# The mean of squares of a delta-rule head: one plain float32 product, or two float32r products of a split pair

## The chip, the cores and the metric

The kernel runs on one core of a Trainium2 chip. The metric is device time of one execution in microseconds (us): the median over runs. One execution was also profiled; its instructions, waits and transfers are the trace. Engines are named as in the profile: PE (TensorE, matrix products), PEld (its weight loads), DVE (VectorE), ACT (ScalarE), POOL (GpSimd) and SP (SyncE, which here issues transfers).

## What is computed

One layer of a sequence model for 1024 tokens and 1024 channels, all in float32:

```
h   = rmsnorm(x);  P = h @ w_in                    # one input projection, its columns cut into parts
A   = gated delta rule, 8 heads of 128 channels, one scan per direction, the directions summed
      -> rmsnorm per head * silu(z) -> w_proj_gdn
B   = gated linear attention, 4 heads, both directions -> rmsnorm per head * silu(g) -> w_proj_gla
out = x + rmsnorm((sigmoid(ga) * A + sigmoid(gb) * B) @ w_out)
```

The change lies in A's norm: for each of the 8 heads and each token, the mean over the head's 128 channels of the squared output, and from it `(mean + eps) ** -0.5`. The 128 channels are on the 128 partitions, so the mean is a product with a 128 x 128 matrix whose every element is 1/128.

## The kernel before

**Stages.** First x is normalised and transposed (to about 60 us). Then come the 8 heads of the delta rule (to about 808 us), during which the next head's projections are computed; then the rest of the gates, the 4 heads of linear attention, the output projections and the last product.

**A head of the delta rule** has these parts, each a function below. `gdn_project` computes k, q and v of a head (products `pj_a`, L251), a convolution over five taps on VectorE (L506, L508) and z (`pj_z`). `gdn_decay` makes the factors `dt`: VectorE makes `xm` (L583), TensorE `pd` (L585) in the two PSUM banks of the pool `pacc`, ScalarE takes the exponential (L588). `gdn_inverse` forms the Gram products (`pgr`, L624), inverts the triangular blocks (a chain of 60 small steps on VectorE, L652 and L654, then small products L683 to L718), and prepares values and `pkq` (L738). `gdn_scan` is the recurrence over 8 chunks in both directions: `psc` (L779, L784, L794) on TensorE, `r`, `vd`, `S` on VectorE (L781, L787, L799), `vn` on ScalarE (L789), and the outputs `po` (L768), which lie in the same two banks as `pd`.

**The end of a scan**, where the change is: ScalarE squares the two halves of 512 tokens of `po` into `o` (L814), VectorE adds them to `osq` (L815), which already holds an eps term from q's norm; `rs_of` takes the mean of each half by a product with `o128` into the banks `s0` and `s1` (L473), then Ln (L478) and, for both halves, Exp (L479). `finish` multiplies z's gate by that root (L125), multiplies the outputs (L465) into `o`, and SP stores it (L466).

`rs_of` has two forms. With `pair` it splits its input: `split` lets ScalarE copy the values to float32r (L163) and VectorE take the difference from the original (L164), and two products of float32r follow (L476, L477). The linear attention uses that form, on halves of 512 tokens. With `None` it makes one product of float32 (L473); the trace shows such a product as two records of the same line. The delta rule uses that form.

**Buffers.** A tile's tag has a fixed number of slots. Tag `qe` has two of 128 x 1024 float32: per head first the queries times the decays of either direction (`qe`: loaded from DRAM, L749, then multiplied by q on VectorE, L750), then the squares `o`, which `finish` overwrites with the output. `pacc` has two banks, used in turn by `pd` of the head after the next and by `po` of the next head. `gt`, with two slots, holds parts of projections on their way to DRAM.

**Order.** The program is written head by head, but a planner orders it when the program is built: it runs a list by priorities (`at(...)`), with its own costs for each instruction, and fixes one order for each engine. An engine then works in that order and waits where an input or a slot is late. Inverse and decay factors come ahead of the scan of the head before, and projections (`P_FILL`) last, so that they fill what is free on TensorE. Beside the last head's scan 13 blocks of gates (`pj_t`) are the filling. SP's transfers, among them the weights (`raw`, L174), also have one order.

Of the kernel before, what the change touches and what calls it, by code (L numbers as in the profile page):

```python
# [32 lines left out]
# tiles of loaded weights, of their split parts, of x normalised, of padded projections  # L33
WRAW, WSPLIT, XS, XP = 2, 4, 4, 3
# the order in which a head's k, q and v are projected
A_ORDER = (1, 0, 2)
# the tiles of x that GpSimd scales, the weights whose low parts it takes
X_POOL = (1, 3, 5, 7)
LO_POOL = "azqv"
# blocks of the first projection's gates that are loaded ahead, and the head after whose states  # L40
GA_AHEAD, GA_HEAD = 2, 2
# gates computed beside a head's scan
# [6 lines left out]
# places in the schedule's order  # L49
# [8 lines left out]
def const_array():  # L58
    """Masks and the like: they depend on shapes alone."""
# [29 lines left out]
def layer_kernel(  # L89
# [23 lines left out]
    @contextmanager  # L113
    def at(priority):
        """what is emitted here comes in the schedule's order from this place on"""
        before = tc.cur_priority
        tc.cur_priority = priority
        yield
        tc.cur_priority = before
# [16 lines left out]
    def mm3(ps, lh, ll, rh, rl, n):  # L136
        """ps = (lh + ll)^T (rh + rl), summed over n pieces, without ll^T rl, which is
        below float32's last place."""
# [4 lines left out]
    # ------------------------------------------------------------ what lives throughout  # L143
# [16 lines left out]
    # ------------------------------------------------------------ split weights, projections  # L160
    def split(src, hi, lo):
        """src as a float32r pair whose sum is exact"""
        nc.scalar.copy(hi, src)  # L163
        nc.vector.tensor_tensor(lo, src, hi.bitcast(F32), op=ALU.subtract)  # L164

    def load_w(src, cols, name, g):
        """part of the rows of columns of a weight, [p, k, n], 512 elements of a partition;
        cols: list of (first column, width, place)."""
# [17 lines left out]
    # the weights' blocks in the order of their use: parts of them are loaded ahead  # L186
# [41 lines left out]
    def project_tokens(name, th, evac):  # L228
        """src^T w for half of the tokens: evac(b, psum) takes [128 tokens, (2 chunks, 256)]"""
        ps = [bank(pj, "pj", f"pj_{name}_{b}") for b in range(2)]  # L230
        for g in range(4):
            hi, lo = next_w(name, g)
            for b in range(2):
                for c in range(2):
                    ts = slice((2 * b + c) * P, (2 * b + c + 1) * P)
                    for k in range(2):
                        kk = 2 * g + k
                        for i, (a, w) in enumerate(((hh, hi), (hl, hi), (hh, lo))):
                            # the first product in a bank clears its marks of what is written
# [6 lines left out]
    def piece(ps, hi, lo, src, th, g, kn, cols=slice(0, 512)):  # L246
        """ps += what the g-th kn pieces of the rows bring, for columns of half of the tokens"""
# [7 lines left out]
    def project(name, evac, src=None):  # L255
        """rows of w^T src: evac(th, psum) takes [channels, 512 tokens]"""
# [8 lines left out]
    def in_steps(name, ps, gn):  # L265
        """as project, by quarters of the tokens"""
# [8 lines left out]
    def project_out(name, dst):  # L275
        """a block of channels kept in DRAM"""
# [13 lines left out]
    # ------------------------------------------------------------ constants of the two mixers  # L290
# [23 lines left out]
    def exp_ln_table():  # L314
        """after a function of another table: the one that has both exp and ln"""
# [4 lines left out]
    # ------------------------------------------------------------ h = rmsnorm(x), transposed  # L320
    with tc.tile_pool(name="xpool", bufs=2) as xpool:
# [23 lines left out]
        def scaled(t):  # L345
            """a tile of x normalised, its transpose"""
# [53 lines left out]
    # ------------------------------------------------------------ decays and gates of the scans  # L400
# [6 lines left out]
    def scan_gates(pool):  # L407
# [17 lines left out]
        # [tokens, direction, head, chunk]  # L425
# [19 lines left out]
        # exp of: the sums up to a token, of what is left of the chunk, of the whole chunk  # L445
# [15 lines left out]
    def finish(o_ps, wcol, rs, zs, o, dst, kc):  # L461
        """o * w * rs * zs, to its place in DRAM; zs is overwritten"""
# [5 lines left out]
    def rs_of(sq, pair, lhsT, eps, name, banks):  # L468
        """sq becomes (mean of sq over the channels + eps) ** -0.5; pair: room for sq as a float32r pair"""
        for i, b in enumerate(banks):  # L470
            pm = bank(*b, f"pm_{name}_{i}")
            if pair is None:
                nc.tensor.matmul(pm, lhsT=lhsT, rhs=sq[:, half(i)], start=True, stop=True)  # L473
            else:
                split(sq[:, half(i)], *pair)
# [678 lines left out]
```

## Time and profile before

| | |
|---|---|
| runs | 1585.59, 1590.22, 1590.51 us; median 1590.22 |
| the profiled execution | span 1591.5 us from its first to its last instruction; no other time of it is given |
| mean granted TensorE clock | 0.982 of full speed |
| busy: PE, PEld, DVE, ACT, POOL | 1526.6, 1283.3, 928.0, 673.1, 201.8 us |

The busy time of an engine is the union of its instructions' times. Products are pipelined, and the ends of their records are modelled, so that records overlap: a stretch of the chain of waits, which counts each moment once, shows how fast they follow one another. In the chain a piece gives its start, its length, the engine, the tile and the line.

### The profile page before, as it was taken

What the parts mean: (1) busy time and instruction counts of PE and PEld (TensorE: products, weight loads), DVE (VectorE), ACT (ScalarE), POOL (GpSimd) and SP (SyncE); (2) the same over time, 40 slices, a digit from 0 to 9 for tenths busy, and PEclk for the clock granted to TensorE, in tenths of its full rate; (3) what the DMA queues carried; (4) which work ended last, traced back from release to release, by engine and by line L of the source; (5) the groups of instructions that cost most, each with busy time, mean ns of one, the idle gap of its engine ahead of it and who ended that gap; (6) DMA issues with size and microseconds to landing.
All of it is one profiled execution on the core that took longest, in us unless ns stands there. A gap on an engine that the chain in (4) does not pass through costs nothing.

```text
span 1591.5 us, 25255 instructions
## 1 busy us (share of the span) xinstructions
PE 1526.6 (96%) x9622; PEld 1283.3 (81%) x9622; DVE 928.0 (58%) x2467; ACT 673.1 (42%) x1370; POOL 201.8 (13%) x225
## 2 busy tenths in 40 slices
PE   6998999999999999999999999999999999999998
PEld 6877787787878878787778898898888988787887
DVE  5497779979999899887511113314323355445413
ACT  5552535343444545453232325525436355433311
POOL 4242112111112121000000120110100100000000
PEclk9998999999999999998999999999999999999999
DMA  5221102121212121024143331231221335655404
GB/s 168 72 73 34 41 28 86 41 73 35 93 34 71 51 81 47 30 81 133 40 142 94 86 75 38 62 79 34 75 59 41 106 89 190 212 169 175 134 27 157
DMA packets 140882, 133.48 MB, mean 84 GB/s; under 512 B 11147, under 2 KB 114875, under 8 KB 140757
## 3 DMA queue, kind: packets, MB, share of 16 engines
q1 hardware_dynamic: 133282, 117.78, 25.0%
q10 hardware_dynamic: 6840, 12.00, 2.5%
q0 software_dynamic: 640, 2.10, 0.4%
q8 instruction: 75, 1.23, 0.3%
q14 instruction: 45, 0.37, 0.1%
HBM read 101.45 MB, written 30.39 MB: 83 GB/s over the span
## 4 chain that ended last, share of the span: by engine, by line
PE 62%; DVE 11%; DMA 6%; ACT 3%; issue 1%; SPq 1%; ACTq 0%; DVEq 0%
PE pj_t L251 9%; PE pj_y L251 7%; PE pj_v L240 6%; PE pout L141 5%; PE pj_a L251 5%; PE pj_g L251 5%; DVE tmp L652 3%; PE pj_q L251 3%; PE pj_k L251 3%; DVE yl L654 3%; PE pj_z L251 2%; PE po L768 2%; PE psb L946 2%; PE pob L968 2%; PE psc L794 1%; DMA st<-ob_d 1%
## 5 line engine op out<-in xcount | busy, mean ns | idle before, releaser
L251 PE MATMUL pj_a<-hh,hi_a 128*128 128x512 f32 x368 | 151.7, 412 | 0.0
L251 PE MATMUL pj_a<-hl,hi_a 128*128 128x512 f32 x368 | 151.0, 410 | 0.0
L251 PE MATMUL pj_a<-hh,lo_a 128*128 128x512 f32 x368 | 150.5, 409 | 0.0
L251 PE MATMUL pj_t<-hh,hi_t 128*128 128x512 f32 x256 | 103.9, 406 | 2.4 <-ACT gt L281 2.4
L251 PE MATMUL pj_t<-hh,lo_t 128*128 128x512 f32 x256 | 104.4, 408 | 0.0
L251 PE MATMUL pj_t<-hl,hi_t 128*128 128x512 f32 x256 | 104.3, 407 | 0.0
L181 POOL TENSOR_TENSOR lo_a<-raw_a,hi_a 128x512 fp32r<-128x512 f32 x48 | 68.6, 1430 | 235.1 <-ACT hi_a L177 224.9
L789 ACT ACTIVATE vn<-psc,c 128x128 f32<-128x128 f32 x128 | 45.0, 366 | 116.4 <-DVE vd L787 88.8
L652 DVE TENSOR_TENSOR tmp<-ulb,yl 128x54 f32<-128x54 f32 (+13 forms) x480 | 93.3, 235 | 1.3 <-DMA yl<-in_consts_dram 1.2
L654 DVE TENSOR_TENSOR yl<-yl,tmp 128x54 f32<-128x54 f32 (+13 forms) x480 | 90.9, 231 | 0.1
L251 PEld LDWEIGHTS pj_a<-hl,hi_a 128*128 128x128 f32 x368 | 71.1, 193 | 12.6 <-issue 1.0
L251 PEld LDWEIGHTS pj_a<-hh,lo_a 128*128 128x128 f32 x368 | 70.6, 192 | 12.8 <-issue 0.7
L251 PEld LDWEIGHTS pj_a<-hh,hi_a 128*128 128x128 f32 x368 | 70.6, 192 | 12.2 <-issue 0.7
L251 PE MATMUL pj_y<-ob,hi_y 128*128 128x512 f32 x256 | 79.1, 390 | 0.9 <-DVE gb L1073 0.9
L141 PE MATMUL pout<-wo,hh 128*128 128x512 f32 (+1 forms) x272 | 79.7, 377 | 0.0
L240 PE MATMUL pj_v<-lo_v,hh 128*128 128x256 f32 x256 | 72.4, 283 | 0.0
L240 PE MATMUL pj_v<-hi_v,hl 128*128 128x256 f32 x256 | 72.4, 283 | 0.0
L240 PE MATMUL pj_v<-hi_v,hh 128*128 128x256 f32 x256 | 72.4, 283 | 0.0
L181 POOL TENSOR_TENSOR lo_v<-raw_v,hi_v 128x512 fp32r<-128x512 f32 x32 | 41.3, 1290 | 231.9 <-ACT hi_v L177 226.1
L183 DVE TENSOR_TENSOR lo_t<-raw_t,hi_t 128x512 fp32r<-128x512 f32 x32 | 22.0, 689 | 64.1 <-ACT hi_t L177 64.0
L251 PEld LDWEIGHTS pj_t<-hh,hi_t 128*128 128x128 f32 x256 | 49.3, 193 | 12.2 <-ACT gt L281 2.8
L141 PEld LDWEIGHTS pout<-wo,hh 128*128 128x128 f32 x272 | 50.1, 188 | 9.4
(313 smaller groups left out, 4071.3 us busy)
## 6 DMA issues: line engine op xcount, KB each, us to landing
raw_a<-in_w_in_dram SPq DMA_DIRECT2D x48, 256.0 KB
qe<-eg_d SPq DMA_DIRECT2D x16, 512.0 KB
raw_t<-in_w_in_dram SPq DMA_DIRECT2D x32, 256.0 KB
gt_d<-gt SPq DMA_DIRECT2D x64, 128.0 KB
raw_v<-in_w_in_dram SPq DMA_DIRECT2D x32, 256.0 KB
xt<-in_x_dram SPq DMA_DIRECT2D x8, 512.0 KB
raw_z<-in_w_in_dram SPq DMA_DIRECT2D x16, 256.0 KB
z_d<-gz SPq DMA_DIRECT2D x32, 128.0 KB
```

Of the source, the lines that this page charges most:

```text
L141: nc.tensor.matmul(ps, lhsT=a(k), rhs=b(k), start=(s == 0), stop=(s == len(steps) - 1))
L181: nc.gpsimd.tensor_tensor(lo, raw, hi.bitcast(F32), op=ALU.subtract)
L183: nc.vector.tensor_tensor(lo, raw, hi.bitcast(F32), op=ALU.subtract)
L240: nc.tensor.matmul(ps[b][:, c * 256:(c + 1) * 256], lhsT=a[th][:, kk, ts], rhs=w[:, k, :], start=kk == 0 and i == 0 and c == 0, stop=kk == ...
L251: nc.tensor.matmul(ps[:, cols], lhsT=a[:, k, :], rhs=b[th][:, kk, cols], start=kk == 0 and a is hi and b is src[0], stop=kk == KD - 1 and ...
L652: nc.vector.tensor_tensor(tv, ul2[:, i, 0:i].unsqueeze(2).broadcast_to([P, i, w_]), yv[:, i].unsqueeze(1).broadcast_to([P, i, w_]), op=ALU ...
L654: nc.vector.tensor_tensor(yv[:, 0:i], yv[:, 0:i], tv, op=ALU.subtract)
L768: nc.tensor.matmul(po_n(n), lhsT=lhsT, rhs=rhs, start=count[b] == 1, stop=count[b] == len(todo[b]))
L789: nc.scalar.mul(vn[d], pc[d][:, P:2 * P], c1[:, d, n:n + 1])
L794: nc.tensor.matmul(pc[d][:, 2 * P:3 * P], lhsT=ktok[:, ns], rhs=vd[d], start=True, stop=True)
L946: nc.tensor.matmul(p_s[:, :256], lhsT=ktok[:, u], rhs=vt[:, n], start=True, stop=True)
L968: nc.tensor.matmul(po[e][:, j * P:(j + 1) * P], lhsT=a, rhs=b, start=(i == 0), stop=(i == len(todo) - 1))
```

## The change

The delta rule's mean is taken by the split form as well. `rs_of` loses its form without a pair. The pair of both halves is one new tile `pr` of tag `qe`: its first 512 columns are the high part and its last 512 the low part, of the first half and then of the second. The output gets a tile of its own, `on`, of the same tag, where before it overwrote the squares. So there are five users of the two slots per head where there were three. The matrix of 1/128 becomes float32r: a memset into a `gt` slot and a copy. The comments of the source are blanked out, which changes nothing that runs; lines below `rs_of` stand three earlier, those behind the end of `gdn_scan` one earlier, and those behind the constant one later.

```diff
     def rs_of(sq, pair, lhsT, eps, name, banks):
         for i, b in enumerate(banks):
             pm = bank(*b, f"pm_{name}_{i}")
-            if pair is None:
-                nc.tensor.matmul(pm, lhsT=lhsT, rhs=sq[:, half(i)], start=True, stop=True)
-            else:
-                split(sq[:, half(i)], *pair)
-                nc.tensor.matmul(pm, lhsT=lhsT, rhs=pair[0], start=True, stop=False)
-                nc.tensor.matmul(pm, lhsT=lhsT, rhs=pair[1], start=False, stop=True)
+            split(sq[:, half(i)], *pair)
+            nc.tensor.matmul(pm, lhsT=lhsT, rhs=pair[0], start=True, stop=False)
+            nc.tensor.matmul(pm, lhsT=lhsT, rhs=pair[1], start=False, stop=True)
             nc.scalar.activation(sq[:, half(i)], pm, AF.Ln, bias=eps_t[eps][:, 0:1])
         return nc.scalar.activation(sq, sq, AF.Exp, scale=-0.5)
...
         o = pool.tile([P, T], F32, tag="qe", name=f"o{h}", bufs=2)
         for g in range(2):
             nc.scalar.activation(o[:, half(g)], po[g], AF.Square)
             nc.vector.tensor_tensor(osq[:, half(g)], osq[:, half(g)], o[:, half(g)], op=ALU.add)
-        rs_of(osq, None, o128, "eq", f"a{h}", ((psc, "s0"), (psc, "s1")))
+        pr = pool.tile([P, T], F32R, tag="qe", name=f"pr{h}", bufs=2)
+        rs_of(osq, (pr[:, half(0)], pr[:, half(1)]), o128, "eq", f"a{h}", ((psc, "s0"), (psc, "s1")))
+        o = pool.tile([P, T], F32, tag="qe", name=f"on{h}", bufs=2)
         finish([(half(g), po[g]) for g in range(2)], gdn_w[:, 0:1], osq, zs[h], o, oa_d, h)
...
-        o128 = mconst.tile([P, P], F32, name="o128")
-        nc.gpsimd.memset(o128, 1.0 / 128)
+        o128 = mconst.tile([P, P], F32R, name="o128")
+        one = gpool.tile([P, 256], F32, name="one128", tag="gt")
+        nc.gpsimd.memset(one, 1.0 / 128)
+        nc.gpsimd.tensor_copy(o128, one[:, :P])
```

## Rows read from the trace of the kernel before

**Rows 1.** The page: span; busy us, share of the span, instructions.

```profile
span 1591.5 us, 25255 instructions
...
PE 1526.6 (96%) x9622; PEld 1283.3 (81%) x9622; DVE 928.0 (58%) x2467; ACT 673.1 (42%) x1370; POOL 201.8 (13%) x225
```

**Rows 2.** Windows of five heads, 268 to 704 us: busy us by engine, summed.

```profile
sum 436.00, PE 416.00 PEld 346.08 DVE 393.09 ACT 202.56 POOL 76.59; mean PE 83.20 PEld 69.22 DVE 78.62 ACT 40.51 POOL 15.32
```

**Rows 3.** TensorE's waits, 268 to 704 us: waited for, us, times, longest.

```profile
PE psc L794 <- ACT vn L789: 7.6, 6, 2.2
PE psc L779 <- DVE S L799: 4.5, 4, 2.2
...
PE pm_a L473 <- DVE osq L815: 1.0, 2, 0.8
PE pd L585 <- DVE o L465: 1.0, 1, 1.0
```

**Rows 4.** Windows of four head ends (394:441, 486:531, 561:612, 657:704), summed.

```profile
sum 190.00, PE 186.02 PEld 152.26 DVE 164.56 ACT 97.81 POOL 36.52; mean PE 46.51 PEld 38.06 DVE 41.14 ACT 24.45 POOL 9.13
```

**Rows 5.** The chain, behind the last head's scan: start, us, engine, tile, line, records.

```profile
802.05 1.99 PE pm_a L473 x4
...
824.59 75.35 PE pj_t L251 x324
```

**Rows 6.** Tile pm_a: count; ns min/median/max; first and last start us.

```profile
L473 PE MATMUL pm_a<-osq,o x32: 590/593/697, 236.6 to 803.4; 128*128 128x512 f32 x32
```

**Rows 7.** Tile pm_b, the same mean in the linear attention.

```profile
L476 PE MATMUL pm_b<-ob_hi,o x8: 394/496/501, 1017.0 to 1333.8; 128*128 128x512 f32 x8
...
L477 PE MATMUL pm_b<-ob_lo,o x8: 419/495/498, 1017.7 to 1335.9; 128*128 128x512 f32 x8
```

**Rows 8.** The chain at the head end of 306 us: the mean's products.

```profile
307.99 1.13 PE pm_a L473 x2
...
311.39 0.86 PE pm_a L473 x2
```

**Rows 9.** Tile ob_hi: the split in the linear attention.

```profile
L163 ACT CAST ob_hi<-sq x8: 615/617/636, 1016.3 to 1332.9; 128x512 fp32r<-128x512 f32 x8
L164 DVE TENSOR_TENSOR ob_lo<-sq,ob_hi x8: 691/692/1419, 1016.9 to 1335.1; 128x512 fp32r<-128x512 f32 x8
```

**Rows 10.** The chain at four head ends: its pieces on VectorE.

```profile
307.44 0.50 DVE osq L815
...
398.18 0.53 DVE osq L815
...
561.55 1.19 DVE k L508
...
562.92 0.60 DVE osq L815
...
737.86 0.75 DVE o L465
```

**Rows 11.** The end of 306 us: timeline, and the chain's load of decayed queries.

```profile
319.49 1.41 DVE L465 SCALAR_TENSOR_TENSOR o<-po,gdn_w,zs 128x512 f32<-128x512 f32 x2
...
325.67 0.48 PE L585 MATMUL pd<-xm,strict 128*128 128x256 f32 x2
...
330.05 4.33 DMA qe<-eg_d
...
341.43 0.38 PE L768 MATMUL po<-qe,S 128*128 128x128 f32 x2
```

**Rows 12.** VectorE's waits, 100 to 820 us.

```profile
DVE qe L750 <- DMA qe<-eg_d: 1.2, 3, 0.5
```

**Rows 13.** SP's waits, 100 to 820 us.

```profile
SPq L466 <- DVE o L465: 39.9, 5, 22.0
```

**Rows 14.** Window with a low clock: us, busy by engine, granted clock, DMA.

```profile
746.00:764.00 18.00, 18.00 (x159) 15.18 (x157) 5.01 (x9) 3.64 (x9) 0.52 (x1) 0.53 0.26 73
```

## The prediction

> **What bounds the kernel now.** I read the page's busy times first, then the windows by head, then what TensorE waits for, then the chain of waits at each head's end, then the tiles of the edited lines.
>
> The page [rows 1] shows TensorE busy for 96% of the span and VectorE for 58%. That mean mixes stages, and every edit but one lies at the ends of the delta rule's heads, so the windows there decide. Over five whole heads, 436 us, TensorE is busy 416.00 us (95%), VectorE 393.09 (90%), ScalarE 202.56 (46%) [rows 2]: two engines are nearly full at once, and TensorE leaves 4 us of the 87 us of a head. Its idle time, 20 us in the five, is mostly the scan's own ping-pong (7.6 and 4.5 us for psc); the mean's addition and the output's multiply hold it 1.0 us each [rows 3]. Four stretches from a scan's end to the next head's Gram products, where the edited code runs, are tighter still: TensorE 186.02 of 190 us (98%), VectorE 164.56 (87%), ScalarE 97.81 (51%) [rows 4]. So the reader is to see that TensorE's own work fills the place of the change, that VectorE has some 6 us of each 47 free there, and that ScalarE has half.
>
> Behind the eighth head's scan TensorE has projections in store (324 products in 75.35 us, merged into one piece of the chain [rows 5]), so a longer chain at that one end is covered.
>
> **The change part by part.** The profiled execution is known by its span, 1591.5 us [rows 1], 1.3 above the median of the runs, 1590.22; differences are worked out inside the span and set on the median.
>
> *Products.* A half head's mean of squares is one plain float32 product, which the trace shows as two records; two halves, four records, take 1.99 us on the path, so 1.00 us a half [rows 5]. It becomes two float32r products of 512 columns. The same shape in the dense stream takes 75.35 / 324 = 0.233 us [rows 5], a pair 0.47. A half gains 0.53 us, the 16 halves 8.5 us of TensorE time. The other bound comes from single records: 0.593 us each for the old ones [rows 6], 0.495 each for the linear attention's hi and lo products [rows 7], a gain of 2 x 0.098 = 0.2 a half, 3.1 in all. I take 0.53, because TensorE runs dense here and the stream is the nearest row. The chain of waits reaches back over the last seven head ends and holds nine of these halves there, the first two at 307.99 and 311.39 [rows 8], the last two in the 1.99 [rows 5]; on it the gain is 9 x 0.53 = 4.8 us.
>
> *Split.* Each half adds a ScalarE copy to float32r and a VectorE subtraction. The same lines at the same shape take 0.617 and 0.692 us in the linear attention [rows 9]: 16 x 0.617 = 9.9 us of ScalarE and 16 x 0.692 = 11.1 of VectorE. ScalarE's are covered by its half-idle time; without that cover they cost up to 9.9. VectorE's cost nothing where TensorE is the path and their whole time where VectorE is. The chain passes through VectorE around these lines at four of the seven ends [rows 10]: at 306 us only the first addition is on it, at 394 the second one leads to the product, at 562 both additions and a conv tap are on it, at 732 the output's multiplies. I count one, one, two and two subtractions: 6 x 0.692 = 4.2 us. At the other ends TensorE is the path. Bounds: 0 and 11.1.
>
> *One pair for both halves.* The second half's copy and subtraction overwrite the pair that the first half's two products read: a new wait of ScalarE and VectorE on TensorE. Behind ScalarE's copy stand the root's Ln and the scan's vn; behind VectorE's subtraction conv taps and the next scan. Its price is at most one product's time a head, 0.495 [rows 7], 4 us over eight, and 0 where other work is placed in between. I take 0, for both queues carry conv, inverse and projection work at that point, and keep 4.
>
> *Buffers.* The tag of the queries' decays has two slots. Now the squares take one, and the next head's first load takes the other at the scan's last step. After the change squares, pair and output come first in the program, so that the first load can wait for the pair's products; the second still waits for the output's store. At the end of 306 us the mean's last product ends at 311.39 + 0.86 = 312.25 [rows 8]; a load takes 4.33 us (330.05 to 334.38), and the scan's first product with a decayed query starts at 341.43 [rows 11]. The first load would land near 317, 24 us early; the second leaves 7 us for its multiply. I take 0. If a multiply stands too early in VectorE's order, the scan waits behind it: at most a landing, 4.3 us a head. VectorE waited for such loads 1.2 us in all [rows 12].
>
> On SP's queue the store stands ahead of weight loads, and SP waited 39.9 us for the output's multiply, at five of eight heads [rows 13]; a later multiply holds those loads by as much. Nothing in TensorE's waits is a weight load [rows 3], so 0.
>
> *The constant.* A memset at the start becomes a memset and a copy, in a slot that the projections' outputs use later. GpSimd does it long before the first mean's product at 236.6 [rows 6]: 0, at most a copy's 0.6 [rows 9].
>
> Sum: -4.8 + 4.2 = -0.6 us; 1590.22 - 0.6 = **1589.6 us**. A difference under 0.3%, 4.8 us, is about what a measurement of this kernel can't tell from no change.
>
> **Rivals.**
>
> *TensorE alone paces it.* If all subtractions fall into VectorE's free time, the whole 8.5 us of TensorE counts: 1581.7. For it: 98% at the head ends [rows 4], and TensorE's larger waits lie in the scan [rows 3]. Against: the VectorE pieces in the chain [rows 10].
>
> *VectorE paces the heads.* Then the 14 subtractions of the first seven ends lengthen them by their whole time, 14 x 0.692 = 9.7, and TensorE only waits longer: 1599.9. For it: 90% over whole heads [rows 2]; it decides once VectorE's 6 us per end are bound in waits for its inputs. Against: those 6 us, beside TensorE's 1.
> The Trainium skill (Perfetto Trace Analysis, "Identifying the Most-Contended Engine") speaks for this rival: matmul busy time is a poor measure of how near TensorE is to its limit, the share of weight loads is to be read instead, while VectorE's busy share may be taken as it is. By that rule TensorE stands at 346.08 of 436 us, 79%, below VectorE's 90% [rows 2], and the change relieves the wrong engine. The trace agrees in part: records of 0.593 us follow one another at 0.50 [rows 5, 6], so busy time overstates each record, though not that no gap is left between them.
>
> *The longer chain holds the decay factors.* The output's multiply frees the two PSUM banks that the decay factors of the head after next (pd) need, and the next scan's outputs wait for pd. Per head the chain gains two copies and two subtractions in series, 2 x 1.31, less 2 x 0.53: 1.6 us, and up to 2.4 more where each subtraction waits for a conv tap of 1.19 [rows 10]. Over six such ends that is 9 to 24 us; with 2 us each, 12: 1602. It decides where the delay exceeds the gap from the multiply's end to pd: 325.67 - 320.90 = 4.8 us at 306 [rows 11], none at 562, where pd waited for the multiply itself [rows 3].
>
> *The change doesn't do what it says.* The order is planned anew, from other product lengths and one more tile. A stretch where TensorE runs at 1.2 instead of 2.4 GHz, as in 746 to 764 us (mean granted clock 0.53 [rows 14], behind the inverse's small products), can come or go: up to half of its 18 us, 1581 to 1599, whatever the products save.
>
> **How the numbers follow.** The forecast, a cancelling, has 0.40: 0.34 of it within 0.3%, 0.04 faster, 0.02 slower. TensorE alone 0.27, faster. VectorE 0.11 and the chain 0.14, slower. The new plan 0.08: 0.04 faster, 0.03 the same, 0.01 slower. Faster 0.04 + 0.27 + 0.04 = 0.35; the same 0.34 + 0.03 = 0.37; slower 0.02 + 0.11 + 0.14 + 0.01 = 0.28. The likeliest case's own range, with 8.5 against nothing and 3.1 against 4.2 with 4 us of waits, is 1582 to 1595. Both signs hold much chance: below, the full 8.5 and half a clock drop, 1577; above, the chain's 12 us, 1603. The chain's far end and a split without any cover are left out.
>
> **What would show it.** The mean's four records of 1.99 us should shrink to under 1; 16 copies near 0.62 and 16 subtractions near 0.69 should appear, VectorE's busy time rising by 11 us. Forecast right: the five heads' 436 us stay within 3. TensorE alone: they shorten by 1 us each. VectorE: it is busy for 90% of longer heads. The chain: the time from the squares to pd grows, and TensorE waits for pd (L585) and the outputs after it. I am wrong if TensorE waits for decayed queries or weights, or if the time moves by over 13 us.

## The result, and the profile after

The kernel after takes 1612.59 us (median of 4 runs, 1610.07 to 1613.91), the kernel before, run beside it, 1589.44. The ratio is 1.014, 95% interval 1.0115 to 1.0165: by it, 22 us slower. The forecast was 1589.6 us, a cancelling of gain and cost; its likeliest range ended at 1595 and its widest at 1603. So it was wrong. In the experiments below, three of the twelve runs with subtractions alone (3793 to 8407 us) and one of the seven with the sum on TensorE (2467 us, the one that was profiled) took far longer than all others and are left out.

The page of the kernel after, its span and busy times (answers to [rows 1]):

```profile
span 1611.8 us, 25310 instructions
...
PE 1534.5 (95%) x9622; PEld 1292.7 (80%) x9622; DVE 937.4 (58%) x2483; ACT 695.2 (43%) x1396; POOL 202.5 (13%) x226
```

TensorE has as many instructions as before and is busy 8 us longer, though its products became shorter. ScalarE has 26 more, and only 16 of them are the copies of the split; the other 10 come up again at the end of the experiments. The windows say why TensorE is busy longer. The two heads in which most is lost, first before, from one head's Gram products to those of the head after next (us; busy by engine; granted clock; DMA share, GB/s):

```profile
440.80:611.70 170.90, 163.17 (x1267) 134.91 (x1266) 156.35 (x491) 79.99 (x175) 34.72 (x40) 1.00 0.20 60
```

and after:

```profile
442.90:626.70 183.80, 174.17 (x1276) 144.74 (x1276) 158.84 (x494) 87.96 (x184) 35.57 (x41) 0.94 0.19 55
```

The two heads take 12.9 us more. The third column from the end is the granted clock: 0.94, a rounded figure, over 183.80 us is 10 to 12 us lost, where before nothing was. So a reader of such a page must look at the clock before the engines' shares: at the lower level the same products take longer, and count as busy (projections of 512 columns follow one another at 0.43 us around 590 us, where the clock is 0.50, and at 0.23 at 600, where it is 1.00).

The instructions that replaced those of [rows 6], by tile, are as forecast in number and length (count; ns min/median/max; first and last start):

```profile
L163 ACT CAST pr<-osq x16: 604/618/628, 233.7 to 820.0; 128x512 fp32r<-128x512 f32 x16
L473 PE MATMUL pm_a<-pr,o x16: 392/398/628, 234.4 to 820.7; 128*128 128x512 f32 x16
L164 DVE TENSOR_TENSOR pr<-osq,pr x16: 679/692/1786, 234.5 to 820.6; 128x512 fp32r<-128x512 f32 x16
L474 PE MATMUL pm_a<-pr,o x16: 391/479/775, 236.3 to 821.4; 128*128 128x512 f32 x16
```

Their order in time isn't. The end of the fifth head in the timeline of the kernel after (start, us, engine, line; in brackets the idle time ahead of it and its releaser):

```profile
586.26 0.62 ACT L163 CAST pr<-osq 128x512 fp32r<-128x512 f32 x1 [0.76 <-DVE osq L812]
587.34 0.68 DVE L164 TENSOR_TENSOR pr<-osq,pr 128x512 fp32r<-128x512 f32 x1
...
590.65 0.63 PE L473 MATMUL pm_a<-pr,o 128*128 128x512 f32 x1
591.32 0.62 ACT L163 CAST pr<-osq 128x512 fp32r<-128x512 f32 x1 [1.35 <-PE pm_a L473]
...
595.64 0.78 PE L474 MATMUL pm_a<-pr,o 128*128 128x512 f32 x1
...
596.52 0.69 DVE L164 TENSOR_TENSOR pr<-osq,pr 128x512 fp32r<-128x512 f32 x1 [0.86 <-PE pm_a L474]
...
599.10 0.48 PE L474 MATMUL pm_a<-pr,o 128*128 128x512 f32 x1
```

The second copy waits for the first high product, the second subtraction for the first low product, and each product stands in TensorE's order behind others. The low half is ready at 588.0 and multiplied only at 595.64, so 9.2 us lie between the two subtractions. This is the longest of the ends, and TensorE ran at half speed from 581.6 to 598.7 us (its row stands in the last section), so part of those 9.2 us is the clock's. From the first square to the end of the output's multiply the first seven heads now take 12.4, 18.8, 19.4, 20.4, 23.8, 17.7 and 17.3 us, some 130 in all, where they took some 100.

TensorE's waits, 100 to 820 us (waited for; us, times, longest), answer to [rows 3] over a wider stretch; before, the largest were 11.7 for vn and 7.2 for xm:

```profile
PE psc L791 <- ACT vn L786: 15.9, 10, 2.4
PE pd L582 <- DVE xm L580: 9.2, 10, 3.1
PE po L765 <- DVE qe L747: 7.1, 1, 7.1
```

The third row is the wait for decayed queries that the prediction had named as a sign of its being wrong.

**One account for all kernels.** What lies behind the first product of the linear attention's queries takes 690 to 695 us in every kernel for which the account is given. Up to it the time splits into TensorE's idle time (the window less its busy time), what the lower clock costs (1 less the mean granted clock, times the span; the lower level is 1.2 of 2.4 GHz, and nearly all such stretches lie there), and the rest, TensorE's work at full clock. The window's row before, and after:

```profile
0.00:900.30 900.30, 847.03 (x5939) 704.82 (x5940) 674.89 (x2035) 392.87 (x838) 151.95 (x183) 0.97 0.24 71
```

```profile
0.00:918.70 918.70, 852.56 (x5939) 713.15 (x5940) 684.33 (x2051) 414.95 (x863) 152.62 (x184) 0.96 0.24 70
```

and the cores' row after, with the mean clock:

```profile
core 0: 1611.8 us, clock 0.974
```

| profiled execution | window | idle | lost to the clock | work at full clock |
|---|---|---|---|---|
| before (clock 0.982) | 900.3 | 53.3 | 28.6 | 818.4 |
| after (0.974) | 918.7 | 66.1 | 41.9 | 810.7 |

By this account the work shrank by 7.7 us, near the 8.5 of the dense stream in [rows 5]; 12.8 us of idle time and 13.3 us of clock stand against it. This split of the time is no finer than some 5 us, though: two kernels below that make the same products differ by 4.6 us in their work at full clock. Over all runs the clock tells the same: its mean is 0.9845 in the 97 runs of the kernel before that stand beside the experiments and 0.9765 in the 4 of the kernel after, that is 24.6 and 37.8 us.

### The profile page after: what moved, and what is told of

Same layout as the page of the kernel before. It is cut to its first block, busy times and chain, and to the rows that moved or that the text cites. A ratio compares the mean times of both kernels' runs of the same rounds, so it can differ in the third digit from the quotient of the medians.

```text
span 1611.8 us, 25310 instructions
## 1 busy us (share of the span) xinstructions
PE 1534.5 (95%) x9622; PEld 1292.7 (80%) x9622; DVE 937.4 (58%) x2483; ACT 695.2 (43%) x1396; POOL 202.5 (13%) x226
## 4 chain that ended last, share of the span: by engine, by line
PE 49%; DMA 5%; DVE 3%; ACT 3%; issue 1%; SPq 0%; ACTq 0%; DVEq 0%
PE pj_t L251 9%; PE pj_y L251 8%; PE pj_v L240 6%; PE pout L141 5%; PE pj_g L251 5%; PE pj_k L251 3%; PE pj_q L251 2%; PE pob L969 2%; PE psb L947 2%; DMA gt_d<-gt 1%; PE pc L901 1%; DMA raw_o<-in_w_out_dram 1%; DVE yl L651 1%; PE po L765 1%; PE pa L932 1%; DVE tmp L649 1%
## 5 line engine op out<-in xcount | busy, mean ns | idle before, releaser
L251 PEld LDWEIGHTS pj_a<-hh,hi_a 128*128 128x128 f32 x368 | 71.9, 195 | 11.5 <-ACT xp L491 0.2
L791 PE MATMUL psc<-vd,ktok 128*128 128x128 f32 x224 | 45.8, 295 | 16.1 <-ACT vn L786 15.9
L791 PEld LDWEIGHTS psc<-vd,ktok 128*128 128x128 f32 x224 | 35.0, 193 | 29.4 <-ACT vn L786 27.0
```

What stands on the lines that cost most here:

```text
L251: nc.tensor.matmul(ps[:, cols], lhsT=a[:, k, :], rhs=b[th][:, kk, cols], start=kk == 0 and a is hi and b is src[0], stop=kk == KD - 1 and ...
L791: nc.tensor.matmul(pc[d][:, 2 * P:3 * P], lhsT=ktok[:, ns], rhs=vd[d], start=True, stop=True)
```

## The experiments

All ratios are to runs of the kernel before beside them; brackets hold 95% intervals.

**Moving the pair out, and the buffers alone.** Four kernels. The first two put the pair into the slots of the keys by tokens:

```diff
-        pr = pool.tile([P, T], F32R, tag="qe", name=f"pr{h}", bufs=2)
+        pr = pool.tile([P, T], F32R, tag="ktok", name=f"pr{h}", bufs=2)
```

in the kernel after, with the output over the squares, and in the kernel before, with a copy and a subtraction of each half that nothing reads.

> The split and its two products as in the changed kernel, but the pair lies in the two slots of the tokens' keys (ktok), and the output overwrites the squares again; so the slots of the decayed queries have three users, as before. If the late loads of the decayed queries (five users of two slots) cost the 20 us: 1583 to 1594, as the split alone gives back TensorE's 8.5 us. If the longer chain in front of the decay factors' banks does: 1604 to 1613, the decay factors again starting where the output's multiply ends. If VectorE's and ScalarE's extra time does: 1604 to 1613 as well, but with the multiply no later after the squares than before.

> The kernel before with the 16 copies and 16 subtractions of the split added in the slots of ktok, at the same place, but nobody reads the pair: the plain product reads the sum as before. If VectorE's and ScalarE's time costs it: 1600 to 1613. If the late loads or the longer chain does: 1588 to 1597.

Measured: 1690.21 us, 1.0641 [1.062, 1.0663], and 1701.35, 1.0716 [1.0668, 1.0763]. Neither expectation was near. In both, the second head's Gram products start 5.6 us after the first head's first square; in the kernel before they start 63 us ahead of it. So the heads no longer overlapped. The slots are handed out in the program's order, and the next head's inverse, which writes its keys there, had to wait for this head's end. The two tell what that overlap is worth, some 100 us, and nothing of the change.

The third gave the kernel before five users of the decayed queries' two slots and no added instruction: the sum goes to a tile of its own, from which the plain product reads, and the output to another.

```diff
-            nc.vector.tensor_tensor(osq[:, half(g)], osq[:, half(g)], o[:, half(g)], op=ALU.add)
+            nc.vector.tensor_tensor(pr[:, half(g)], osq[:, half(g)], o[:, half(g)], op=ALU.add)
...
+        o = pool.tile([P, T], F32, tag="qe", name=f"on{h}", bufs=2)
```

> The kernel before with the five users of the two slots alone: the sum of squares is written to a tile in a slot of the decayed queries, the plain float32 product reads it there, and the output has a tile of its own. No instruction is added. If the late loads cost it: 1600 to 1613. If the longer chain or the added engine time does: 1586 to 1594.

Measured: 1589.32 us, 1.0005 [0.9987, 1.0024], idle time 53.3 us and clock 0.982 as before. That is in the range for the longer chain or the engines' time: the slots alone cost nothing. Its order of instructions was planned anew too, and differs from that of the kernel before in many places, so a new order by itself need not cost either.

The fourth gave the decay factors other banks in the kernel after, those of the Gram products:

```diff
-                pd = bank(pacc, f"o{g}", f"pd{h}_{d}_{g}")
+                pd = bank(pg, "g", f"pd{h}_{d}_{g}")
```

> The changed kernel, but the decay factors' products go to the two general PSUM banks (pg), so that they need not wait for the output's multiply; the next scan's outputs still do. If the longer chain in front of the decay factors costs it: 1585 to 1598. If the late loads do: 1603 to 1613, the scan's first outputs still standing behind the second load's multiply. If engine time does: 1603 to 1613 too, without such a wait.

Measured: 1625.58 us, 1.0228 [1.0199, 1.0256], slower still and outside both ranges. The factors no longer need the output's multiply, but they now share the inverse's banks; inconclusive.

**The split's work, and the chain's length.** From the kernel before, the copies and subtractions are added over the squares' buffer, read by nothing; then the subtractions alone.

```diff
+        for g in range(2):
+            hi = o[:, half(g)].bitcast(F32R)
+            split(osq[:, half(g)], hi, hi)
```

> The kernel before with the split's 16 copies and 16 subtractions added at the same place, now over the squares' own buffer (both parts into the same half, nobody reads them), so that no slot is shared in another way than before; the plain product reads the sum as before. If the engines' added time costs the 22 us: 1602 to 1614. If the longer chain up to the decay factors' banks does: 1588 to 1597.

> From the kernel before, with the 16 subtractions on VectorE alone added over the squares' buffer, not read by anything (no copies on ScalarE). With copies and subtractions both it was 1596.99 us, 9 above the kernel before. Theory 'VectorE's time costs it': 1594 to 1598 us. Rival 'ScalarE's time costs it': 1588 to 1590 us.

Measured: 1596.99 us, 1.0064 [1.0045, 1.0083], and 1593.77, 1.0023 [1.0004, 1.0043]. The first lies at the upper end of the range for the longer chain and below that for the engines' time; the second lies between its two ranges, nearer to VectorE's. The subtractions cost 3.7 us (0.0023 of 1590), the copies some 6 on top, though the intervals all but touch. So ScalarE's half-idle time was no full cover. Nor is this engine time alone: the output's multiply writes over the same buffer and has to wait for the idle split.

Then only the length of the chain: a GpSimd copy of each half between sum and plain product.

```diff
+            nc.gpsimd.tensor_copy(o[:, half(g)], osq[:, half(g)])
```

> The kernel before with nothing on VectorE and ScalarE, but with GpSimd copying each half of the sum over the squares before the plain product reads it from there: the chain gets longer by some 1.5 to 3 us a head. If the longer chain costs it: 1598 to 1614. If the engines' added time does: 1586 to 1593.

Measured: 1609.68 us, 1.0134 [1.0098, 1.017], inside the range for the longer chain. So a chain made longer, with no pair, no shared buffer and nothing added to VectorE or ScalarE, can cost as much as the whole change. But its seven ends lengthened by 10.4 us in all, those of the kernel with idle splits by 20.7, which lost half as much: the length of an end doesn't tell the time.

**Who pays for the pair.** The high part alone (the mean is that of the rounded squares, the low part is left out), then a pair for each half, with six users of the two slots:

```diff
-            split(sq[:, half(i)], *pair)
-            nc.tensor.matmul(pm, lhsT=lhsT, rhs=pair[0], start=True, stop=False)
-            nc.tensor.matmul(pm, lhsT=lhsT, rhs=pair[1], start=False, stop=True)
+            nc.scalar.copy(pair[i], sq[:, half(i)])
+            nc.tensor.matmul(pm, lhsT=lhsT, rhs=pair[i], start=True, stop=True)
```

```diff
+        pl = pool.tile([P, T], F32R, tag="qe", name=f"pl{h}", bufs=2)
+        rs_of(osq, [(pr[:, half(g)], pl[:, half(g)]) for g in range(2)], o128, "eq", f"a{h}", ((psc, "s0"), (psc, "s1")))
```

> The changed kernel without the low part: one copy to float32r and one product per half, halves in their own places (the mean of the squares is then taken of rounded squares). TensorE saves 0.77 us a half, no subtraction, no wait of the second half for the first. If the chain through the subtraction and the shared pair costs it: 1578 to 1592. If the late loads do, with ScalarE's copy: 1600 to 1610. If VectorE's time does: 1578 to 1592 too, which f2 and f5 tell apart.

> The changed kernel with a pair for each half (high parts in one tile, low parts in another, six users of the two slots): same instructions, but the second half's split does not wait for the first half's products, which stand behind the inverse's products in TensorE's order. If that wait makes the chain long: 1586 to 1600, the decay factors starting 3 to 6 us sooner after the scan. If the chain is long by the split itself or the engines' time costs it: 1604 to 1614.

Measured: 1581.37, 0.9958 [0.9937, 0.9978], and 1599.15, 1.0059 [1.0035, 1.0082]. Both are where the theory of the shared pair had them. The second does the change's whole computation, with no wait for a buffer of the first half, and most of the loss is gone. The same place in its timeline, here at full clock:

```profile
574.81 1.14 ACT L163 CAST pr<-osq 128x512 fp32r<-128x512 f32 x2
575.47 1.29 DVE L164 TENSOR_TENSOR pl<-osq,pr 128x512 fp32r<-128x512 f32 x2
...
579.79 0.71 PE L475 MATMUL pm_a<-pl,o 128*128 128x512 f32 x2
```

Both copies, both subtractions and both low products now run as pairs.

Next, the last head. In the kernel after its loads of the decays are issued at 785.78 us behind the next layer's transfers, and the 7.1 us of waiting follow. Issued from ScalarE's queue instead, with the shared pair and with a pair for each half:

```diff
-            nc.sync.dma_start(qe, eg_d[d, h:h + 1, :].broadcast_to([P, T]))
+            (nc.scalar if h == HA - 1 else nc.sync).dma_start(qe, eg_d[d, h:h + 1, :].broadcast_to([P, T]))
```

> The kernel after, with one thing changed: the eighth head's two loads of the queries' decays are issued from ScalarE's queue, so that they don't stand on SP's queue behind the next layer's transfers (in the trace of the kernel after they are issued at 785.78 us, behind transfers that wait for the step before; the product po of the last head waits 7.1 us for the multiply of the decayed queries, and the granted clock is low for 10.2 us after 786.4). Theory 'the late loads of the last head are one piece of the loss': about 1603 to 1606 us, the wait of po for the decayed queries gone and the stretch of low clock at 786 us gone. Rival 'the whole loss lies in the shared pair, this wait only moves idle time that is lost anyway': 1610 to 1614 us.

> The kernel after with a pair of its own for each half (six users of the queries' decays' buffers) and the last head's two loads issued from ScalarE's queue. If both pieces are there and add (13 us from the shared pair, about 9 from the late loads), the whole loss of 22 us is given back: 1587 to 1593 us. If the late loads are no piece of their own: 1597 to 1600 us, as with the pair for each half alone (1599.15).

Measured: 1611.15, 1.0142 [1.0115, 1.0169], and 1595.19, 1.0022 [1.0001, 1.0043]. The wait shrank to 3.0 us and the total did not move (1.014 before it): that theory fell. The second lies between its two ranges; with it, two kernels without sharing are at 1.0022 and 1.0059.

Now one index apart from the pair for each half: the high parts apart, one low part for both halves.

```diff
-        rs_of(osq, [(pr[:, half(g)], pl[:, half(g)]) for g in range(2)], o128, "eq", f"a{h}", ((psc, "s0"), (psc, "s1")))
+        rs_of(osq, [(pr[:, half(g)], pl[:, half(0)]) for g in range(2)], o128, "eq", f"a{h}", ((psc, "s0"), (psc, "s1")))
```

> The kernel after with a high part of its own for each half (ScalarE's second copy waits for no product), while both halves still share one low part (VectorE's second subtraction waits for the first half's low product). Same six users of the decayed queries' two buffers as with a pair for each half. If sharing the low part costs, through VectorE's wait: 1603 to 1611 us. If only ScalarE's wait on the high part costs (6 us for the high part alone, 1589.04 against 1581.37): 1592 to 1600 us, as with a pair for each half.

Measured: 1610.6 us, 1.0117 [1.0094, 1.0139], as expected if sharing the low part costs. The program has the same instructions and the same users of the slots; only the second subtraction must wait for the first low product. That is 0.0058 above the pair for each half, 9 us. The planned orders differ more than the edit: ScalarE runs 1396 instructions here, as in the kernel after, and 1388 with a pair for each half. Its window and the other's, and their clocks:

```profile
0.00:917.00 917.00, 849.23 (x5938) 709.20 (x5939) 683.87 (x2051) 414.26 (x863) 151.55 (x184) 0.96 0.24 70
```

```profile
core 0: 1612.0 us, clock 0.977
```

```profile
0.00:893.60 893.60, 832.62 (x5938) 692.85 (x5939) 684.96 (x2051) 403.71 (x855) 149.34 (x184) 0.98 0.24 72
```

```profile
core 0: 1585.3 us, clock 0.990
```

Idle time 67.8 against 61.0 us, the clock's loss 37.1 against 15.9, work at full clock 812.1 against 816.7. (This profiled execution of the pair for each half is its fastest; over all runs the mean clocks are 0.9798 and 0.9857, 32.4 against 22.8 us, 9.6 of the 11.5 between the medians.) So most of these 9 to 11 us are paid in clock, not in waits.

The counterpart, one high part for both halves, without a low part:

```diff
-                nc.scalar.copy(pair[i], sq[:, half(i)])
-                nc.tensor.matmul(pm, lhsT=lhsT, rhs=pair[i], start=True, stop=True)
+                nc.scalar.copy(pair[0], sq[:, half(i)])
+                nc.tensor.matmul(pm, lhsT=lhsT, rhs=pair[0], start=True, stop=True)
```

> The high part alone, but both halves use one buffer of 512 columns, so that the second half's copy on ScalarE waits for the first half's product (in the form that gave 1581.37 us each half has its own). If ScalarE's wait on a shared buffer is what the shared pair costs: 1588 to 1600 us. If it is the wait of VectorE's subtraction, or the length of the whole chain of two copies and two subtractions: 1580 to 1585 us.

Measured: 1589.04, 0.9997 [0.9979, 1.0014]; 0.0039 or 6 us above its form with two buffers and inside the range for a shared buffer, with intervals that just miss each other (0.9978 and 0.9979). Sharing costs there too, and takes the form's whole gain.

**Where the longer chain binds.** In the trace of the kernel after, the decay factors start at the very end of the output's multiply at all six ends that such factors follow, which speaks for the rival of the longer chain; but with a pair for each half they do so too, and most of the loss is gone there. The multiply can be taken off the chain at no cost in instructions: `finish_early` multiplies the outputs by the weight and z's gate as soon as the squares are summed, over the squares, which frees the banks; `finish_late` multiplies by the root and stores.

```diff
+        finish_early([(half(g), po[g]) for g in range(2)], gdn_w[:, 0:1], zs[h], o)
...
-        finish([(half(g), po[g]) for g in range(2)], gdn_w[:, 0:1], osq, zs[h], o, oa_d, h)
+        finish_late(osq, o, oa_d, h)
```

> From the kernel before, with the output's multiply taken apart: as soon as the squares are added up, VectorE multiplies the scan's outputs by the weight and by z's gate, out of PSUM and over the squares, and multiplies by the root afterwards, in SBUF. The number of VectorE's instructions is the same; the two PSUM banks that the decay factors of the head after next need come free before the mean's product instead of behind its whole chain. Theory 'the loop of banks paces the heads' (scan's outputs, squares, mean, root, output's multiply, decay factors, next scan's outputs): in the kernel before the decay factors start at the very end of the multiply at three or four of seven ends, so some of the loop is bound there too: 1575 to 1586 us. Rival 'the engines' queues pace the heads, the loop has slack': 1588 to 1594 us.

> The kernel after, split and one shared pair and two float32r products as they are, with the output's multiply taken apart in the same way (the output lies over the squares again). Theory 'the loop of banks': the pair's chain is no longer in the loop, and most of the 22 us is given back: 1580 to 1595 us. Rival 'the waits of ScalarE's and VectorE's queues for the shared pair hold what stands behind them': those waits stay, 1606 to 1614 us.

> The high part alone (a copy and one float32r product a half, the mean is that of rounded squares; 1581.37 us before) with the output's multiply taken apart in the same way. Theory 'the loop of banks': as the kernel before with the early multiply, less the products' saving, 1568 to 1580 us. Rival 'the queues': no gain from it, 1579 to 1586 us.

Measured: 1580.57, 0.9945 [0.9927, 0.9963] from the kernel before; 1603.22, 1.0105 [1.0065, 1.0145] from the kernel after; 1579.29, 0.9938 [0.9916, 0.996] with the high part alone. The first is as the theory of the banks had it; the second lies between its two ranges; the third fits either. The early multiply is worth 9 us to the kernel before. It gives the kernel after no more than that, and 1.05% of loss stays, 1.6% against the kernel before with the same edit: the banks aren't where the change costs. Another loop came into view. Rows of SP and VectorE in the timeline of the kernel after with the early multiply:

```profile
517.28 0.32 SPq L474 DMA_DIRECT2D oa_d<-o  x1
...
523.59 0.38 SPq L754 DMA_DIRECT2D qe<-eg_d  x1
...
529.08 1.23 DVE L755 TENSOR_TENSOR qe<-qe,q 128x1024 f32<-128x1024 f32 x1 [3.82 <-DMA qe<-eg_d]
```

The next head's second load waits for the store, VectorE for the load, and the scan's small steps stand behind; TensorE waited 11.7 us for decayed queries. The last multiply's output was therefore put over z's gate, so that the slot comes free at 517 instead of with the store's landing:

```diff
-        pool_mul(o, rs, o)
-        nc.sync.dma_start(dst[:, kc], o)
+        pool_mul(zs, rs, o)
+        nc.sync.dma_start(dst[:, kc], zs)
```

> The kernel after with the early multiply (1603.22 us), and the last multiply by the root writes the output into z's gate, from where it is stored; so the decayed queries' buffer that held the output comes free at that multiply instead of at the store's landing. In the trace with the early multiply the second load of the decayed queries is issued only when the store has landed (523.59 us, the store issued at 517.28), VectorE waits 3.82 us for it, and the scan's small steps stand behind that. Theory 'a loop through the two buffers of the decayed queries (pair, output, store, load, multiply by q, next scan) paces the heads': 1588 to 1598 us. Rival 'the waits of ScalarE and VectorE on the shared pair': 1601 to 1606 us, as without it.

Measured: 1612.47 us, 1.0128 [1.0107, 1.015]. Neither expectation held. TensorE's waits for decayed queries fell from 11.7 to 1.3 us and most scans, from the first output's product to the first square, from some 70 to 59, but the time did not fall: TensorE now waits 21.6 us for vn (9.0 before that edit), and the profiled execution has 63.5 us of idle time and 45.0 us lost to the clock (0.972). So this isn't the cause either.

**The sum on TensorE.** Squares and eps term as float32r, added up by two products, with no VectorE sum, copy or subtraction (the mean is that of rounded operands).

```diff
+            nc.tensor.matmul(pm, lhsT=o128, rhs=osq[:, half(g)], start=True, stop=False)
+            nc.tensor.matmul(pm, lhsT=o128, rhs=o[:, half(g)], start=False, stop=True)
```

> From the kernel before: ScalarE writes the squares and the other term of the sum as float32r, and two float32r products on TensorE add them up into the mean, in place of VectorE's sum and the plain float32 product; no copy and no subtraction. The mean is that of operands rounded to float32r. Theory 'what the plain products cost on TensorE is saved once nothing is added to VectorE's and ScalarE's part of the chain': 1575 to 1583 us, as the high part alone gave (1581.37) or better, since VectorE's sum (16 of them) goes too. Rival 'the head's chain is paced by the engines of the scan, not by the products': 1586 to 1590 us.

Measured: 1599.11 us, 1.0061 [1.0038, 1.0083]. Both expectations failed, and why stays open: each of its parts was to save time, and there is no trace of a run like these. It has no split and no pair, so a plan made anew can cost some 10 us without either.

**What ScalarE's 10 other instructions are.** They are loads of function tables (`ACT_TABLE_LOAD`, 1.283 us each): 48 in the kernel after, 38 before. The rows of the kernel after that have more than before (busy us, mean ns):

```profile
L486 ACT ACT_TABLE_LOAD x7 | 9.0, 1283 | 0.1
L585 ACT ACT_TABLE_LOAD x6 | 7.7, 1283 | 0.0
```

Before, the same lines have 2 and 1. At five heads the table of Silu has just been loaded when some of the decay factors' Exp (L585) follow in the new order, so that Exp's table is loaded back, and then Silu's once more (L486): 12.8 us of ScalarE, more than the copies' 9.9. The kernels with the shared low part and the output's multiply as it was have 48 loads, those with a pair for each half 40. So the contrasts between these two groups hold 8 loads, 10.3 us of ScalarE, beside the shared buffer, and no run tells the two apart. The loads are not needed for such a loss: with the early multiply there are 38, and 1.0105 to 1.0128 is lost.

## Why the prediction was wrong

**Products: not contradicted, but not measured by themselves.** TensorE's work at full clock fell by 7.7 us, between the bounds 3.1 and 8.5. With a pair for each half, which makes the same products, it fell by only 1.7 (818.4 to 816.7). The high part alone gains 0.42%, but it leaves the low products out.

**Split: too low.** I took 4.2 us within 0 and 11.1. Subtractions alone cost 3.7, as I had counted; copies and subtractions together 10 (0.0064). ScalarE's copies, put at 0, were the miss, though part of the 10 may be the output's multiply, which stood behind the idle split. And I counted 9.9 us on ScalarE; it became busy for 22.1 more, because the new order has ten more table loads.

**Buffers: the slots cost 0**, as taken (1.0005). What I did not see is that with the pair the first load must wait for a chain that itself had become longer. TensorE then waited 7.1 us for decayed queries, which I had named as a sign; but moving the loads and freeing a slot earlier both shortened that wait and not the time, so it isn't the loss.

**One pair for both halves: the step that failed.** I took 0 and kept 4 us: "at most one product's time a head", and nothing "where other work is placed in between". The waits themselves came to that: in the kernel after VectorE stood 1.7 us and ScalarE 2.1 us before the shared pair was free. What I had at nothing is the other work: the planner put it between, and the waiting subtraction and the product behind it were each put behind it, as at 587 to 599 us. A pair for each half takes back 0.0081 to 0.0118 of the loss, 13 to 19 us; the shared low part alone costs 9, a shared high part, in its own form, 6. Without the sharing the change comes out at 1.0022 to 1.0059, 3.5 to 9.4 us of loss, about 1594 to 1600 us: near and above the upper end of the "cancelling", 1595. The split's 10 us less the 4.8 that I took for the products, 5 us, lie in that. That the sharing costs is shown as far as these orders go; that it costs by the work in between is argued from the timeline.

**The rival of the longer chain** had the direction right, and its sign in the trace, the factors at the multiply's end; its price reached 24 us, and the GpSimd copy shows that a longer chain alone can cost 21. The five heads of [rows 2], from the third head's Gram products to the eighth's, take 447.2 us instead of 435.4, as it had it; but with the buffers alone they take 445 at an unchanged total, so that window, which I had named as the test, doesn't tell. And with the banks freed early the loss stays at 1.0105 to 1.0128, while the same edit takes 0.55% from the kernel before: what it removes was there already, and the change adds little to it. The rival's condition, the banks, is not where the loss is; that the longer chain costs in some other way is not ruled out.

**VectorE paces the heads:** in the two worst heads VectorE is busy for 158.84 of 183.80 us, 86%, against 156.35 of 170.90, 91%. It is no fuller; 10 to 12 of the 12.9 us lost there are the clock's. By the rule of the Trainium skill (Perfetto Trace Analysis, "Identifying the Most-Contended Engine"), which reads weight loads against VectorE, VectorE is the limit in both (weight loads 79% in either); the trace agrees that TensorE's busy time misleads, but not that VectorE's share tells the loss.

**The new plan and the clock** I had at 0.08, as a chance of either sign, with a drop of the clock as its price. The clock is how half the loss is paid: 13 us. What stays open is the last link, how one wait between two halves becomes many short gaps and clock drops over a head. Each kernel was ordered anew, and none of the experiments held the order fixed. The engines' idle time at the shared pair is small in the kernel after, as VectorE's row tells (waited for; us, times, longest):

```profile
DVE pr L164 <- PE pm_a L474: 1.7, 5, 0.9
```

ScalarE waits much longer for the mean's last product, ahead of Ln. Before, after, and with a pair for each half:

```profile
ACT osq L478 <- PE pm_a L473: 5.1, 10, 2.1
ACT osq L475 <- PE pm_a L474: 16.7, 10, 4.5
ACT osq L476 <- PE pm_a L475: 18.1, 8, 3.3
```

But that wait is as long with a pair for each half, where most of the loss is gone. So a queue that stands still isn't the answer. What is shown is that five kernels with the shared low part (after, last loads moved, high parts apart, and both early multiplies) lie at 1.0105 to 1.0142, and two with a pair for each half at 1.0022 and 1.0059. The moves of the pair into the keys' slots and of the decay factors into other banks, costly by themselves, are left aside. Against it stand the kernels that lose without any pair, 1.0134 with the GpSimd copy and 1.0061 with the sum on TensorE: a plan made anew, or a longer chain, can cost as much, and only an order held fixed would tell how much of the 13 to 19 us is the shared buffer's own.

## What to carry to other kernels

Give each piece of a split its own buffer before counting what the split saves: a buffer shared by two halves turns parallel pieces into a chain, and a planner that fills its gaps with other work can make each link several times as long as the instruction in it. Count the instructions of every engine after the change: ten more than expected on ScalarE were on the first page here. Where two engines are nearly full, split a change's loss into idle time, granted clock and work before looking for a wait to blame; here the work did not grow and the loss was in the other two. And an output multiply that can be done ahead of the root is worth doing ahead: with no added instruction the kernel before takes 0.9945 of its time; with the high part alone as well it is 0.9938, which is no measurable difference.

## What the runs showed of the hardware

A drop of the clock does not need an idle engine. In the kernel after, TensorE is busy for 13.49 of the 13.60 us ahead of the longest one, then runs 17.1 us at half speed:

```profile
568.00:581.60 13.60, 13.49 (x198) 11.79 (x197) 11.41 (x35) 6.18 (x15) 1.88 (x4) 1.00 0.12 32
581.60:598.70 17.10, 17.10 (x116) 14.21 (x114) 8.89 (x13) 5.45 (x11) 0.00 (x0) 0.50 0.01 2
```

Of those 198 products 139 are the inverse's 32 x 32 ones and 23 are long projections of 512 columns. The same part of the kernel with a pair for each half, with 160 and 25 of 217, kept the full clock:

```profile
557.00:572.00 15.00, 14.55 (x217) 11.92 (x216) 14.43 (x33) 5.63 (x15) 1.97 (x4) 1.00 0.08 20
```

So neither the busy time nor the mix of products tells the two stretches apart, and what set the drop is not shown. But the runs of one kernel differ by it, too: those with the early multiply from the kernel after lie between 1598.08 us at a mean clock of 0.985 and 1616.01 at 0.975, 18 us for a difference of 0.010, which is 16 us of the span.
